# FFN up product as seven block products in a diffusion backbone layer

## Chip, cores and metric

One Trainium2 chip, one core. The time is the device time of one execution in microseconds (us). The kernel before took 1220.67 us, the median of three runs (1220.33 to 1224.66).

## What is computed

One layer on 1024 latent tokens of width 1024, with 256 context tokens. A token mixer comes first: an input projection, then three groups of heads in parallel (a bidirectional state-space scan, a Fourier mix and a pooling mix), and an output projection. A ConvFFN follows. Both are joined to the residual and normalised. The part that the change is about:

```python
def conv_ffn(h, w_up, conv_w, conv_b, w_down, grid):
    a = h @ w_up                                  # 1024 x 1024 @ 1024 x 5632
    a = dwconv2d_grid(a, conv_w, conv_b)          # 3 x 3 per channel on a 16 x 64 grid of tokens
    val, gate = jnp.split(a, 2, axis=-1)          # 2816 channels each
    return (jax.nn.gelu(gate) * val) @ w_down

x = post_norm(x, mix_lat, g1, ln1_g[l], ln1_b[l])
ffn_lat = conv_ffn(modulate(x, sh2, sc2), ...)
x = post_norm(x, ffn_lat, g2, ln2_g[l], ln2_b[l])   # LN(alpha * x + gate * y)
```

In the scan, a chunk of 128 tokens needs, for each of 8 heads and both directions, a 128 x 128 matrix of decays, exp of the difference of two cumulative sums, masked to a triangle and multiplied by C B^T and by dt.

## The kernel before, in words

All products are done in two-part arithmetic: an operand is split into a high part of fewer mantissa bits and a low remainder, and a product is three matmuls, high x high, high x low and low x high. `split` (L214) does it: ScalarE (ACT) writes the high part and GpSimd (POOL), or VectorE (DVE) if named, subtracts to get the low part.

The mixer fills the first 400 us. For every chunk and group of four heads `chunk_pre` (L610) forms C B^T in PSUM, masks it into two triangles (`gt`, L618), multiplies each by dt per head (`U`, L620 and L641), loads the cumulative sums broadcast over partitions (`bc`, L627), subtracts this partition's sum for the two directions and takes the minimum of both (`E`, L629 to L640), takes exp (L642), multiplies (L643) and stores the matrix to DRAM. Output projection, first normalisation (`post1`, L1070) and the transposed, modulated and split input of the FFN (`post2`, L1086) follow. That input lies in SBUF as `h2h` and `h2l`: two halves of 512 tokens, 8 feature tiles of 128.

The FFN goes over 22 channel pairs, each a value tile and a gate tile of 128 channels (L1216). For one tile the weights are loaded and split by `up_weights` (L1119), and 8 features x 3 products x 2 halves = 48 matmuls of 128x512 go into a 128x1024 PSUM tile (L1229). `conv2d` (L1164) takes it from PSUM: one ACT operation for the centre tap and eight DVE operations for the other taps (L1180). After the gate tile come gelu (ACT), the product with the value (POOL) and its split (L1247 to L1249), and the load and split of the pair's rows of the down matrix (L1250 to L1254).

The down product runs between the up products. For every two finished pairs there are 16 units (`down_unit`, L1144), one for each of 8 token tiles and two halves of the output width: 6 matmuls into a 128x512 PSUM tile, whose sum DVE adds to the residual `xa`, which stays in SBUF (L1157, L1159). A unit is put behind every second feature of an up tile (L1231). Nine groups of 16 make 144 units; the last four pairs are a last group, which is multiplied after the last up tile, token tile by token tile (`last_mm`, L1268), and normalised as it is finished (`post_early`, `post_late`).

PSUM has three tiles of 128x1024 (`psa`: the up tiles, later the last group) and two of 128x512 (`psb`: the units). The text gives dependencies and a priority; the order on each engine is fixed ahead of time by a planner that takes what is ready by its own estimates, and at run time each engine keeps that order and waits where an operand isn't there. All DMAs are issued by SyncE (SP), in one queue.

Of the kernel before, what the change touches and what calls it, by code (L numbers as in the profile page):

```python
# [33 lines left out]
def hybrid_layer(  # L34
# [179 lines left out]
    def split(raw, hi, lo, eng=None):  # L214

        S.activation(hi, raw, AF.Identity)  # L216
        (eng or G).tensor_tensor(lo, raw, hi.bitcast(F32), op=ALU.subtract)  # L217
# [262 lines left out]
    dtv, etot, ecs, ncs = (d3(n) for n in ("dtv", "etot", "ecs", "ncs"))  # L480
# [12 lines left out]
    def decay_a(dct):  # L493
# [23 lines left out]
        V.tensor_tensor(dA, dtv, b10(nea[:]), op=ALU.mult)  # L517
        dts.update(dA=dA, cs=cs, tot=tot)

    def decay_b():  # L520
# [12 lines left out]
        V.tensor_scalar(ncs, cs, -1.0, None, op0=ALU.mult)  # L533
# [73 lines left out]
    t12 = mat[:, 1:3, :]  # L607
    ms = nc.dram_tensor("m_scratch", [NT, P, 1024], F32, kind="Internal").ap()

    def chunk_pre(ch, g):  # L610
# [6 lines left out]
        gt = sl.tile([P, 2, P], F32, tag="gt", name=f"gt{ch}{g}")  # L617
        V.tensor_tensor(gt, pg[:, 0:P].unsqueeze(1).broadcast_to([P, 2, P]), t12, op=ALU.mult)  # L618
        f = g * 8
        V.tensor_tensor(U, gt[:, 0, :].unsqueeze(1).broadcast_to([P, 4, P]),  # L620
                        dtv[:, ch, f : f + 4].unsqueeze(2).broadcast_to([P, 4, P]), op=ALU.mult)
        for h in range(4):
            f, b = g * 8 + h, g * 8 + 4 + h
            if h % 2 == 0:
                bc = half("bc", f"bc{ch}{g}{h}", [P, 2, 2, P])
                r = scr[ch * 16 + f : ch * 16 + f + 1, :]
                nc.sync.dma_start(bc, bass.AP(r.tensor, r.offset, [[0, P], [4 * P, 2], [P, 2], [1, P]]))  # L627
                if g == 0:
                    G.tensor_tensor(E[:, h : h + 2, :], bc[:, 0],  # L629
                                    ncs[:, ch, f : f + 2].unsqueeze(2).broadcast_to([P, 2, P]), op=ALU.add)  # L630
                else:
                    for i in range(2):
                        S.activation(E[:, h + i, :], bc[:, 0, i, :], AF.Identity, bias=ncs[:, ch, f + i : f + i + 1])
            if g == 1:
                V.scalar_tensor_tensor(E[:, h, :], bc[:, 1, h % 2, :], ncs[:, ch, b : b + 1], E[:, h, :], op0=ALU.add,  # L635
                                       op1=ALU.min)
            else:
                S.activation(bc[:, 1, h % 2, :], bc[:, 1, h % 2, :], AF.Identity, bias=ncs[:, ch, b : b + 1])
                if h % 2:
                    V.tensor_tensor(E[:, h - 1 : h + 1, :], E[:, h - 1 : h + 1, :], bc[:, 1], op=ALU.min)  # L640
            V.scalar_tensor_tensor(U[:, h, :], gt[:, 1, :], dtv[:, ch, b : b + 1], U[:, h, :], op0=ALU.mult, op1=ALU.add)  # L641
        S.activation(E, E, AF.Exp)  # L642
        G.tensor_tensor(U, U, E, op=ALU.mult)  # L643
# [244 lines left out]
    def chunk_y(ch):  # L888
# [6 lines left out]
                        dcol.unsqueeze(2).broadcast_to([P, 8, 64]), op=ALU.mult)  # L895
# [170 lines left out]
    nc.sync.dma_start(a2r, adar[8:24, :])  # L1066
    xnc = cycle(lambda n: qt("q10", n), lambda n: qt("q11", n), lambda n: post.tile([P, D], F32, tag="p0", name=n))


    def post1(t):  # L1070
# [3 lines left out]
        V.scalar_tensor_tensor(xa[t], xa[t], st[1], lnb, op0=ALU.mult, op1=ALU.add)  # L1074
        st = ln_stats([xa[t]], f"ln2_{t}")
# [51 lines left out]

# [16 lines left out]
    def down_unit(u):  # L1144

        group, t, nb = u
        pt = psb(f"pdn{group[0][0]}_{t}_{nb}")
        n = 3 * len(group)
        i = 0
        s = slice(nb * 512, nb * 512 + 512)  # L1150
        for _, gh, gl, wh, wl in group:
            a, b = gh[:, t * P : (t + 1) * P], gl[:, t * P : (t + 1) * P]
            for u_, v_ in ((a, wh), (a, wl), (b, wh)):
                TE.matmul(pt, u_, v_[:, s], start=i == 0, stop=i == n - 1)  # L1154
                i += 1
        if (t, nb) in seen:
            V.tensor_tensor(xa[t][:, s], xa[t][:, s], pt, op=ALU.add)  # L1157
# [57 lines left out]
    group, queue, acc_v = [], [], None  # L1215
    for n in range(NCT):  # L1216
        ct, i = chan[n], n // 2
        if n > 1 and n + 1 < NCT:
# [192 lines left out]
```

## Time and profile before

| | |
|---|---|
| median of three runs | 1220.67 us |
| the profiled execution | 1225.25 us, span 1223.5 us, mean granted clock 0.983 |
| busy | PE 1158.4, DVE 967.7, POOL 466.3, ACT 383.4 us |
| instructions | PE 5463, DVE 1388, ACT 572, POOL 243 |
| DMA | 122.51 MB |

The profile is one execution. PE is TensorE's matmuls, PEld its weight loads. A row of a timeline gives the start, the time of the merged group, the engine, the line, the operation, the tiles out<-in with their shapes, the count, and in brackets the idle time before it and what ended that. A row of groups gives busy time, mean time of one, and idle time before.

### The profile page before, as it was taken

Reading aid. Unit: us, or ns where it says so; the run is one execution under the profiler, and the core shown is the slowest. Engines: PE = TensorE matmul, PEld = TensorE weight load, DVE = VectorE, ACT = ScalarE, POOL = GpSimd, SP = SyncE. Lnnn points to the kernel's source line nnn. Section 1 sums busy time; section 2 is a strip of 40 time slices with the busy share of each in tenths; the row PEclk is TensorE's granted clock in tenths of the full one; section 3 lists DMA queues with packets and bytes.
Section 4 is the critical chain, followed back from the end, with each engine's and each line's share of the span. In section 5 each row is a group of like instructions: output and inputs, shape, how many; then the busy total and the mean of one; then the engine's idle time right before and its main releaser. Section 6 shows DMA issues by size and latency. Waiting matters only on the chain.

```text
span 1223.5 us, 14330 instructions
## 1 busy us (share of the span) xinstructions
PE 1158.4 (95%) x5463; PEld 941.2 (77%) x5463; DVE 967.7 (79%) x1388; ACT 383.4 (31%) x572; POOL 466.3 (38%) x243
## 2 busy tenths in 40 slices
PE   4999998989978998999999999999999999999996
PEld 2698886767856787788888888888888888888884
DVE  4788799999899889798777777777777777777957
ACT  2263466721443133342221222211222212222144
POOL 0010143353344034674343535343443535353146
PEclk9999998998989999999999999999999999999998
DMA  9848455566526111222021211121121112121013
GB/s 311 293 145 314 156 167 167 162 207 212 198 84 209 43 36 52 69 70 63 24 69 35 69 33 54 35 69 36 35 69 35 52 35 69 35 69 35 18 35 138
DMA packets 104779, 122.51 MB, mean 100 GB/s; under 512 B 7021, under 2 KB 83579, under 8 KB 104711
## 3 DMA queue, kind: packets, MB, share of 16 engines
q1 hardware_dynamic: 104711, 121.60, 31.0%
q8 instruction: 43, 0.70, 0.2%
q14 instruction: 25, 0.20, 0.1%
HBM read 106.82 MB, written 14.76 MB: 99 GB/s over the span
## 4 chain that ended last, share of the span: by engine, by line
PE 75%; DVE 15%; issue 4%; DMA 3%; ACT 1%; POOL 1%; SPq 0%; DVEq 0%; ACTq 0%; POOLq 0%
PE pu L1229 37%; PE pdn L1154 16%; PE pout L1004 4%; PE px L443 4%; PE pz L342 4%; PE pl L1278 3%; PE pu L1190 1%; DVE EU L641 1%; DMA wa<-in_w_ada_dram 1%; DVE EU L635 1%; PE pd L906 1%; DVE st L706 1%; PE pp L443 1%; DVE EU L620 1%; DVE xa L1073 1%
## 5 line engine op out<-in xcount | busy, mean ns | idle before, releaser
L1180 DVE SCALAR_TENSOR_TENSOR cv<-pu,ffc,cv 128x945 f32<-128x945 f32 (+7 forms) x368 | 432.6, 1177 | 20.6 <-ACT cv L1172 10.9
L1229 PE MATMUL pu<-h2l,wuh 128*128 128x512 f32 x656 | 205.6, 394 | 0.0
L1229 PE MATMUL pu<-h2h,wuh 128*128 128x512 f32 x656 | 205.5, 394 | 0.0
L1229 PE MATMUL pu<-h2h,wul 128*128 128x512 f32 x656 | 205.0, 394 | 0.0
L1157 DVE TENSOR_TENSOR xa<-xa,pdn 128x512 f32<-128x512 f32 x128 | 87.4, 683 | 129.0 <-PE pdn L1154 128.7
L217 POOL TENSOR_TENSOR wul<-wur,wuh 128x1024 fp32r<-128x1024 f32 x44 | 106.8, 2427 | 205.1 <-ACT wuh L216 205.1
L1229 PEld LDWEIGHTS pu<-h2h,wul 128*128 128x128 f32 x656 | 123.1, 188 | 29.2
L1229 PEld LDWEIGHTS pu<-h2l,wuh 128*128 128x128 f32 x656 | 123.2, 188 | 29.0
L1229 PEld LDWEIGHTS pu<-h2h,wuh 128*128 128x128 f32 x656 | 123.3, 188 | 28.8
L216 ACT ACTIVATE wuh<-wur 128x1024 fp32r<-128x1024 f32 x44 | 46.3, 1054 | 240.6 <-PE pu L1229 221.8
L1154 PE MATMUL pdn<-wdh,gl 128*128 128x512 f32 x288 | 113.2, 393 | 0.0
L1154 PE MATMUL pdn<-wdl,gh 128*128 128x512 f32 x288 | 113.1, 393 | 0.0
L1154 PE MATMUL pdn<-wdh,gh 128*128 128x512 f32 x288 | 112.8, 392 | 0.0
L1252 POOL TENSOR_TENSOR wdr<-wdr,g2b 128x1024 f32<-128x1024 f32 x22 | 53.0, 2408 | 68.0 <-DMA wdr<-in_ffn_w_down_dram 68.0
L1248 POOL TENSOR_TENSOR cv<-cv,cv 128x1024 f32<-128x1024 f32 (+1 forms) x23 | 53.0, 2306 | 60.4 <-ACT cv L1247 60.3
L217 POOL TENSOR_TENSOR gl<-cv,gh 128x1024 fp32r<-128x1024 f32 (+1 forms) x23 | 53.3, 2317 | 42.4 <-ACT gh L216 42.4
L1154 PEld LDWEIGHTS pdn<-wdl,gh 128*128 128x128 f32 x288 | 54.0, 188 | 12.5
L1154 PEld LDWEIGHTS pdn<-wdh,gh 128*128 128x128 f32 x288 | 54.0, 188 | 12.4
L1154 PEld LDWEIGHTS pdn<-wdh,gl 128*128 128x128 f32 x288 | 54.0, 188 | 12.1
L1172 ACT ACTIVATE cv<-pu,ffc 128x1024 f32<-128x1024 f32 (+3 forms) x46 | 53.1, 1155 | 29.5 <-PE pu L1229 19.3
L1247 ACT ACTIVATE cv<-cv 128x1024 f32<-128x1024 f32 (+1 forms) x23 | 23.5, 1020 | 120.2 <-DVE cv L1180 120.2
L217 POOL TENSOR_TENSOR wdl<-wdr,wdh 128x1024 fp32r<-128x1024 f32 x22 | 52.8, 2415 | 4.7 <-ACT wdh L216 4.7
(351 smaller groups left out, 2124.5 us busy)
## 6 DMA issues: line engine op xcount, KB each, us to landing
wur<-in_ffn_w_up_dram SPq DMA_DIRECT2D x44, 512.0 KB
wad<-in_w_ada_dram SPq DMA_DIRECT2D x32, 512.0 KB
wdr<-in_ffn_w_down_dram SPq DMA_DIRECT2D x22, 512.0 KB
wa<-in_w_ada_dram SPq DMA_DIRECT2D x32, 256.0 KB
bc<-cs_scratch SPq DMA_DIRECT2D x32, 256.0 KB
xr<-in_x_dram SPq DMA_DIRECT2D x8, 512.0 KB
wx_r<-in_w_in_dram SPq DMA_DIRECT2D x8, 512.0 KB
m_scratch<-EU SPq DMA_DIRECT2D x16, 256.0 KB
```

Source lines behind the costliest of these rows:

```text
L216: S.activation(hi, raw, AF.Identity)
L217: (eng or G).tensor_tensor(lo, raw, hi.bitcast(F32), op=ALU.subtract)
L342: TE.matmul(pt[:, j * 512 : j * 512 + ZW], a, b[:, k % 4, :], start=first and i == 0, stop=last and i == 2)
L443: TE.matmul(pt[:, q * 512 : q * 512 + 512], a[:, k, :], b[q][:, k, :], start=k == 0 and i == 0, stop=k == KD - 1 and i == 2)
L1004: TE.matmul(pt[:, nb * 512 : nb * 512 + 512], u, v[:, nb * 512 : nb * 512 + 512], start=first and i == 0, stop=last and i == 2)
L1154: TE.matmul(pt, u_, v_[:, s], start=i == 0, stop=i == n - 1)
L1157: V.tensor_tensor(xa[t][:, s], xa[t][:, s], pt, op=ALU.add)
L1172: S.activation(acc[:, a * 64 : b * 64], pt[:, a * 64 : b * 64], AF.Identity, bias=ffc[:, 396 + ct : 397 + ct], scale=ffc[:, 176 + ct : 177 ...
L1180: last = V.scalar_tensor_tensor(dst, pv[:, r0 + dy : r1 + dy, c0 + dx : c1 + dx], ffc[:, w * 44 + ct : w * 44 + ct + 1], dst, op0=ALU.mult ...
L1229: TE.matmul(pt[:, q * 512 : q * 512 + 512], a[:, k, :], b[q][:, k, :], start=k == 0 and j == 0, stop=k == KD - 1 and j == 2)
L1248: G.tensor_tensor(acc[:, s], acc[:, s], acc_v[:, s], op=ALU.mult)
L1252: G.tensor_tensor(raw, raw, g2b, op=ALU.mult)
```

## The change

From pair 5 on, the up product of a pair is done by Strassen's scheme on six of the eight feature tiles. The 2 x 2 blocks are value and gate channels on one side, features 5 to 7 and 2 to 4 on the other, and the two halves of 512 tokens. Seven block products of 3 features take the place of eight; features 0 and 1 are multiplied as before. The sums of blocks of weights are made by POOL from the raw weights and split (`pair_sums`); those of the input are made once by DVE during pairs 1 to 3 (`combine`) and split, three of them into tiles of their own and the fourth in place of features 5 to 7 of the second half of tokens (`last_t4`). The products are chained in PSUM: ACT copies a partial sum from one bank into another, and later products are added on top of it. Only the seventh product has a PSUM tile of its own, is copied to SBUF and added by DVE.

```diff
+    def first_product(i):
+        pv[i] = psa(f"pu{chan[2 * i]}")
+        X, Z = pv[i][:, 0:512], pv[i][:, 512:1024]
+        mm(X, wk(vw[i], K1), hk(0, K1), True)
+        S.copy(Z, X)
+
+    def pair(i, mid):
+        if i not in pv:
+            first_product(i)
+        X, Z = pv[i][:, 0:512], pv[i][:, 512:1024]
+        mm(X, wk(vw[i], K2), hk(0, K2))
+        slot()
+        mm(Z, sk(i, 2), tk(2))
+        pq[i] = psa(f"pu{chan[2 * i + 1]}")
+        Y, W_ = pq[i][:, 0:512], pq[i][:, 512:1024]
+        S.copy(Y, Z)
+        mm(X, wk(vw[i], 0, KD0), hk(0, 0, KD0))
+        slot()
+        p7 = psb(f"p7_{i}")
+        mm(p7, sk(i, 3), tk(3), True)
+        s7 = post.tile([P, 512], F32, tag="s7", name=f"s7_{i}")
+        S.copy(s7, p7)
+        slot()
+        mm(Z, sk(i, 1), tk(1))
+        seed = S.copy(W_, Z)
...
+        mm(Y, wk(gw[i], K2), hk(1, K1))
+        mm(Z, sk(i, 4), hk(1, K2))
+        if i + 1 < NPAIR:
+            pair_sums(i + 1)
+        mm(Z, wk(vw[i], 0, KD0), hk(1, 0, KD0))
+        slot()
+        acc_v = conv2d(pv[i], chan[2 * i], [(0, 16)])
+        mid()
+        if i + 1 < NPAIR:
+            first_product(i + 1)
+        slot()
+        mm(Y, wk(gw[i], 0, KD0), hk(0, 0, KD0))
+        slot()
+        mm(W_, wk(gw[i], 0, KD0), hk(1, 0, KD0))
...
+        V.tensor_tensor(pqv, pqv, s7.unsqueeze(1).broadcast_to([P, 2, 512]), op=ALU.add)
+        return acc_v
```

`mm` does the three matmuls of each feature into one bank; `slot` puts in one down unit if there is one. Direct pairs keep four slots a tile, a Strassen pair has eight, from pair 3 to the last. The sums of weights and of the input:

```diff
+    def combine(k):
...
+        whole(b11, 0, K1 + k)
+        whole(b12, 1, K1 + k)
+        whole(b22, 1, K2 + k)
+        whole(b21, 0, K2 + k)
+        eng().tensor_tensor(b11, b12, b11, op=ALU.subtract)
+        eng().tensor_tensor(b12, b22, b12, op=ALU.subtract)
+        eng().tensor_tensor(b22, b22, b11, op=ALU.subtract)
+        eng().tensor_tensor(b21, b21, b22, op=ALU.subtract)
+        for j, src in ((0, b11), (1, b22), (2, b12)):
+            split(src, Tt[j][k][:, 0, :], Tt[j][k][:, 1, :], eng())
...
+    def pair_sums(i):
...
+        G.tensor_tensor(a21, a21, a22, op=ALU.add)
+        G.tensor_tensor(a11, a21, a11, op=ALU.subtract)
+        split_s(i, 2, a11)
+        split_s(i, 1, a21)
+        G.tensor_tensor(a12, a12, a11, op=ALU.subtract)
+        split_s(i, 4, a12)
+        G.tensor_tensor(a11, a22, a11, op=ALU.subtract)
+        split_s(i, 3, a11)
```

To make room in SBUF the residual moves to DRAM: `post1` stores it, each unit loads its 128x512 piece into one of three buffers and stores it back, and it is loaded whole for the last group. The down weights are loaded and split in halves of the output width, and the gated product of a pair is formed one pair later (`between`), in two halves.

```diff
     def down_unit(u):
 
         group, t, nb = u
+        xt = post.tile([P, 512], F32, tag="xt", name=f"xt{group[0][0]}_{t}_{nb}", bufs=3)
+        xs = xd[t * P : (t + 1) * P, nb * 512 : nb * 512 + 512]
+        nc.sync.dma_start(xt, xs)
...
         if (t, nb) in seen:
-            V.tensor_tensor(xa[t][:, s], xa[t][:, s], pt, op=ALU.add)
+            V.tensor_tensor(xt, xt, pt, op=ALU.add)
         else:
-            V.scalar_tensor_tensor(xa[t][:, s], xa[t][:, s], ALPHA, pt, op0=ALU.mult, op1=ALU.add)
+            V.scalar_tensor_tensor(xt, xt, ALPHA, pt, op0=ALU.mult, op1=ALU.add)
             seen.add((t, nb))
+        nc.sync.dma_start(xs, xt)
```

In the mixer, the logarithm of dt is put into the exponent, so that `U` needs no products with dt; the lower triangle is chosen by a predicated copy in place of the minimum, and the diagonal is handled with the skip connection. The constant matrices are loaded in two pieces.

```diff
     def chunk_pre(ch, g):
...
+        gt = sl.tile([P, P], F32, tag="gt", name=f"gt{ch}{g}", bufs=2)
+        V.tensor_copy(gt, pg[:, 0:P])
+        gd = sm.tile([P, 1], F32, tag="gd", name=f"gd{ch}{g}")
+        V.scalar_tensor_tensor(junk, pg[:, 0:P], 1.0, ident, op0=ALU.mult, op1=ALU.mult, accum_out=gd)
+        f = g * 8
+        V.scalar_tensor_tensor(skip[:, ch, g * 4 : g * 4 + 4], dtv[:, ch, f + 4 : f + 8], gd, dcol[:, g * 4 : g * 4 + 4],
+                               op0=ALU.mult, op1=ALU.add)
...
+                G.tensor_tensor(bc[:, 1], bc[:, 1], ncs[:, ch, b : b + 2].unsqueeze(2).broadcast_to([P, 2, P]), op=ALU.add)
+            S.activation(E[:, h, :], bc[:, 0, h % 2, :], AF.Identity, bias=ncs[:, ch, f : f + 1])
+            if h % 2:
+                V.copy_predicated(E[:, h - 1 : h + 1, :], below.bitcast(later).unsqueeze(1).broadcast_to([P, 2, P]), bc[:, 1])
         S.activation(E, E, AF.Exp)
-        G.tensor_tensor(U, U, E, op=ALU.mult)
+        V.tensor_tensor(U, E, gt.unsqueeze(1).broadcast_to([P, 4, P]), op=ALU.mult)
         nc.sync.dma_start(ms[ch][:, g * 512 : g * 512 + 512], U.rearrange("p a b -> p (a b)"))
```

More of the change, by code (lines that the diff above doesn't have):

```diff
@@ L478, in b10 @@
         return ap.unsqueeze(1).broadcast_to([P, 10, 16])
-    dtv, etot, ecs, ncs = (d3(n) for n in ("dtv", "etot", "ecs", "ncs"))
+    dtv, etot, ecs, ncs, ldt = (d3(n) for n in ("dtv", "etot", "ecs", "ncs", "ldt"))
     nea = sl.tile([P, 16], F32, name="nea")
@@ L1214, in hybrid_layer @@
     utags = cycle(("wh0", "wl0"), ("wh1", "wl1"))
[L1215 to L1218, printed above, removed]
[L1219 to L1243 removed]
+    TTAG = iter(("q0", "q1", "q8", "q9", "q12", "q14", "q2", "q3", "q4"))
@@ new lines, in pair_gate, with mm @@
+    def pair_gate(i):
+        n = KD - KS
+        wh, wl = qt("X0", f"gwh{i}", [P, n, P], F32R), qt("EM1", f"gwl{i}", [P, n, P], F32R)
+        g = raws.pop(i)[1]
+        split(g[:, 0:n, :], wh[:], wl[:])
+        gw[i] = wh, wl
+    def mm(dst, a, b, start=False):
+        n = len(a)
+        for k in range(n):
+            for j, (u, w) in enumerate(((0, 0), (0, 1), (1, 0))):
+                TE.matmul(dst, a[k][u], b[k][w], start=start and k == 0 and j == 0, stop=k == n - 1 and j == 2,
+                          skip_group_check=True)
@@ L1249, in hybrid_layer @@
             split(acc[:, s], gh[:, s], gl[:, s])
-        raw = ring("ht2", f"wdr{i}")
-        nc.sync.dma_start(raw, w_down[i * P : (i + 1) * P, :])
-        G.tensor_tensor(raw, raw, g2b, op=ALU.mult)
-        wdh, wdl = qt(tg[2], f"wdh{i}", dt=F32R), qt(tg[3], f"wdl{i}", dt=F32R)
-        split(raw[:], wdh[:], wdl[:])
-        group.append((i, gh, gl, wdh, wdl))
-        if len(group) == 2 and i < NPAIR - 3:
-            queue = [(list(group), t, nb) for t in range(NT) for nb in range(2)]
-            group = []
+        gates[i] = gh, gl
@@ new lines, in hybrid_layer, with between @@
+    LASTG = NPAIR - 4
+    accs_ = {}
+    def between(i):
+        j = i - 1
+        if j < 0:
+            return
+        gated(j, *accs_.pop(j))
+        if j < LASTG:
+            if j % 2 == 1:
+                grp = [(m, *gates[m], wds[m]) for m in (j - 1, j)]
+                units.extend((grp, t, nb) for nb in range(2) for t in range(NT))
+                for m in (j - 1, j):
+                    down_raw(m, 1)
+            else:
+                for m in (j, j + 1):
+                    down_raw(m, 0)
+        else:
+            for m in {LASTG: (0,), LASTG + 1: (1,)}.get(j, ()):
+                down_raw(LASTG, m)
+                down_raw(LASTG + 1, m)
@@ L1264, in hybrid_layer @@
         down_unit(u)
+    for t, tag in enumerate(STAG + ("X0", "EM1", "q4", "wh0")):
+        xa[t] = qt(tag, f"xl{t}")
+        nc.sync.dma_start(xa[t], xd[t * P : (t + 1) * P, :])
+    down_split()
+    LT = iter(("q0", "q1", "q8", "q9"))
+    for m in range(LASTG + 2, NPAIR):
+        for nb in range(2):
+            down_weights(m, nb, next(LT))
+    gated(NPAIR - 1, *accs_.pop(NPAIR - 1), tags=("q12", "q14"))
+    group = [(m, *gates[m], wds[m]) for m in range(LASTG, NPAIR)]
     NG = len(group)
```

213 lines of the change are left out of this document (148 added, 65 removed).

## The prediction

> **What bounds the kernel now.** I read the page's chain of waits, then a table of stretches, then the PE and DVE timelines of the FFN, and last the two places where PE is not full.
>
> ```profile
> PE 75%; DVE 15%; issue 4%; DMA 3%; ACT 1%; POOL 1%; SPq 0%; DVEq 0%; ACTq 0%; POOLq 0%
> ```
>
> PE is three quarters of the chain that sets the end. The table of stretches says where (columns: window, length, then PE, PEld, DVE, ACT, POOL busy with instruction counts, granted clock, DMA share, GB/s):
>
> ```profile
> 140.00:205.00 65.00, 60.83 (x311) 51.45 (x310) 59.35 (x95) 39.69 (x66) 21.49 (x21) 0.95 0.62 194
> 205.00:290.00 85.00, 76.01 (x367) 60.86 (x365) 83.59 (x169) 37.17 (x71) 38.86 (x35) 0.98 0.60 194
> 290.00:400.00 110.00, 93.07 (x465) 76.50 (x466) 98.62 (x163) 42.42 (x109) 39.10 (x20) 0.92 0.48 163
> 511.00:1155.00 644.00, 644.00 (x2783) 522.17 (x2782) 487.76 (x470) 150.44 (x143) 287.57 (x120) 1.00 0.17 50
> ```
>
> From 511 to 1155 us, the FFN, PE never idles, at full clock; DVE has 24% to spare and the DMA engines 83%. From 140 to 400 us, the mixer, DVE is the fuller engine (241.6 of 260 us) and PE idles 30 us. So a matmul taken out of the FFN is worth its whole price as long as nothing new makes PE wait, and DVE work taken out of the mixer is worth something, at most PE's idle time.
>
> **The price of a matmul, and the count.** Two timelines of the FFN, PE and DVE:
>
> ```profile
> 801.55 0.63 PE L1229 MATMUL pu<-h2h,wuh 128*128 128x512 f32 x2
> ...
> 804.32 0.40 PE L1154 MATMUL pdn<-wdh,gh 128*128 128x512 f32 x1
> ...
> 805.71 0.63 PE L1229 MATMUL pu<-h2h,wuh 128*128 128x512 f32 x2
> ```
>
> ```profile
> 810.68 3.69 DVE L1180 SCALAR_TENSOR_TENSOR cv<-pu,ffc,cv 128x945 f32<-128x945 f32 x3
> 814.29 0.68 DVE L1157 TENSOR_TENSOR xa<-xa,pdn 128x512 f32<-128x512 f32 x1
> 814.88 3.80 DVE L1180 SCALAR_TENSOR_TENSOR cv<-pu,ffc,cv 128x1008 f32<-128x1008 f32 x3
> 818.60 0.68 DVE L1157 TENSOR_TENSOR xa<-xa,pdn 128x512 f32<-128x512 f32 x1
> 819.20 2.45 DVE L1180 SCALAR_TENSOR_TENSOR cv<-pu,ffc,cv 128x960 f32<-128x960 f32 x2
> ```
>
> From 801.55 to 805.71 PE does 12 up matmuls and the 6 of one down unit: 4.16 / 18 = 0.231 us each. The six of a unit go to one bank one after another (804.32 to 805.71, 1.39 / 6 = 0.232), so the new chains, nine in a row into one bank, should cost no more apiece. A pair now has 2 tiles x 8 features x 3 x 2 halves = 96 up matmuls. A Strassen pair has 7 products x 3 features x 3 = 63, and 4 blocks x 2 remaining features x 3 = 24: 87. Pairs 5 to 21 are Strassen: 17 x 9 = 153 matmuls fewer, 153 x 0.231 = **-35.4 us**. The 144 down units and the last group keep their matmuls. With 8 units (48) a Strassen pair lasts 135 x 0.231 = 31.2 us instead of 33.3.
>
> **Does the rest of a pair fit in 31.2 us?** In the second timeline eight taps last 3.61 + 3.72 + 2.45 = 9.8 us and a unit's sum delays the taps by 0.60; sums are slipped between taps as they become ready, so the order on an engine is by readiness, not by the text. Prices for the rest:
>
> ```profile
> 1174.28 1.29 POOL L217 TENSOR_TENSOR gl<-cv,gh 128x512 fp32r<-128x512 f32 x1 [0.74 <-ACT gh L216]
> ...
> 1179.51 2.41 POOL L217 TENSOR_TENSOR wdl<-wdr,wdh 128x1024 fp32r<-128x1024 f32 x1
> ```
>
> ```profile
> 1185.19 1.22 DVE L1301 TENSOR_TENSOR xa<-xa,pl 128x1024 f32<-128x1024 f32 x1 [12.24 <-PE pl L1278]
> ```
>
> ```profile
> 1194.22 0.57 ACT L1290 COPY pl<-xa 128x512 f32<-128x512 f32 x1
> ```
>
> DVE per pair: 2 x 9.8 + 8 x 0.60 + 1.2 for adding the seventh product = 25.6 us (82%). POOL: eight 128x384 operations (about 1.0 each between the two rows), value low part 2.4, gate low part about 1.6, four halves of down weights and four of the gated product at 1.29: 22.4 us (72%). Neither is the bound. The four PSUM copies on ACT are new waits. Each is bounded below by 0 and above by its copy, 0.57 us and a hand-off, where nothing stands between; but six to thirty matmuls (1.4 to 7 us) stand between each copy and the matmul that needs its bank again. Behind a late copy on ACT wait the other copies and the splits. The tight place is the two-buffer PSUM ring: the third unit of a pair takes the buffer of the second with only the nine matmuls of the seventh product between, 2.1 us, while its sum needs a hand-off of 0.2, the rest of a tap (up to 1.2) and 0.68. That is 0 to 0.6 us a pair; with 0.3, the middle, **+5 us** over 17 pairs (bounds 0 and 10).
>
> **Residual in DRAM.** Each unit gets a 256 KB load and a 256 KB store on SP's queue, 16 more issues a pair. Rows for a 512 KB load (issue, then the operation that waited for it), for a store and for a slow load:
>
> ```profile
> 578.67 0.34 SPq L1251 DMA_DIRECT2D wdr<-in_ffn_w_down_dram  x1
> ```
>
> ```profile
> 582.45 2.40 POOL L1252 TENSOR_TENSOR wdr<-wdr,g2b 128x1024 f32<-128x1024 f32 x1 [3.80 <-DMA wdr<-in_ffn_w_down_dram]
> ```
>
> ```profile
> 189.88 5.17 DMA wf_r<-in_w_in_dram
> ...
> 271.17 2.00 DMA m_scratch<-EU
> ```
>
> Issue to use was 3.8 us, for twice the bytes; a store cost 2.0. A buffer's round is 3.8 + 0.68 + 0.34 + 2.0 = 6.8 us; there are three, and the closest three units of a pair lie 39 matmuls, 9.0 us, apart. So I cost it at nothing: the ring hides it. Traffic: 4 MB a pair is some 130 GB/s on top of 50, where the mixer moved 194 at a 0.62 share. The store of x in the first normalisation adds eight 512 KB issues behind DVE work near 450 us, where DMA is nearly idle: nothing, or 0.34 us each. The split constant and the few small operations on dt (128x160, each under the 0.41 us of L618 below): nothing to 1 us.
>
> **Changeover to Strassen.** The combinations of features are 36 DVE operations on 128x512 (33 in pairs 1 to 3, then 3 that split T4 in place, after the last direct tile). DVE is behind in those pairs already:
>
> ```profile
> 503.16 47.38 DVE L1180 SCALAR_TENSOR_TENSOR cv<-pu,ffc,cv 128x504 f32<-128x504 f32 x41 [4.68 <-ACT cv L1172]
> ```
>
> ```profile
> 609.29 1.19 ACT L1172 ACTIVATE cv<-pu,ffc 128x1024 f32<-128x1024 f32 x1
> ```
>
> It runs taps without a gap from 503. Tile 9, the last direct one, is done at 609.3, with one unit more before it at 610.7. T4 is needed 66 matmuls and one uncovered copy later: 627. DVE until then: 503.2 + 6.0 (rest of tile 0) + 9 x 9.8 + 16 x 0.60 = 607, plus 36 operations. At 0.60 that ends at 628.5; but these read two SBUF operands, and the mixer's groups by line (busy us, mean ns) show what that costs beside POOL:
>
> ```profile
> L641 DVE SCALAR_TENSOR_TENSOR EU<-gt,dtv,EU 128x128 f32<-128x128 f32 x64 | 24.0, 414 | 0.1
> ...
> L620 DVE TENSOR_TENSOR EU<-gt,dtv 128x512 f32<-128x512 f32 x16 | 14.4, 898 | 0.1
> L635 DVE SCALAR_TENSOR_TENSOR EU<-bc,ncs,EU 128x128 f32<-128x128 f32 x32 | 12.1, 414 | 0.0
> L640 DVE TENSOR_TENSOR EU<-EU,bc 128x256 f32<-128x256 f32 x16 | 9.6, 604 | 3.5 <-ACT cvc L558 1.7 <-POOL EU L629 1.0 <-ACT bc L638 0.9
> L618 DVE TENSOR_TENSOR gt<-pg,mat 128x256 f32<-128x256 f32 x16 | 6.6, 414 | 0.1
> L706 DVE TENSOR_TENSOR st<-st,etot 128x512 f32<-128x512 f32 x7 | 5.9, 843 | 0.4 <-DMA m_scratch<-EU 0.4
> ...
> L709 DVE TENSOR_TENSOR st<-st,pst 128x512 f32<-128x512 f32 x7 | 4.6, 677 | 0.0
> ```
>
> The same 128x512 size takes 843 ns with two SBUF operands (L706) and 677 with one in PSUM (L709): 0.17 more, so 0.77 each, ending at 634.5. PE waits **+7 us**; bounds 1 (no contention) and 21 (first rival). The Trainium skill, "SBUF — State Buffer", section "SBUF: two separate sides", says that such a DVE operation and a GpSimd one exclude each other for the whole instruction. This rule speaks against the change: by it the time is the first rival's.
>
> **Mixer.** Lines 641, 620, 635, 640 and 618 above are what a chunk's preparation costs DVE, and they all go: 24.0 + 12.1 + 9.6 + 6.6 + 14.4 = 66.7 us. In their place, sixteen times: a 128x128 copy (under L618's 0.41), a 128x128 product with a sum (0.41), a tiny one (under 0.2), two predicated copies of 128x256 and one 128x512 product (0.90 as L620). No row shows a predicated copy: 0.42 if like L618, 0.60 if like L640, both of its size; I take 0.5, the middle. About 2.8 in all, 16 x 2.8 = 45 us: DVE is relieved of 22, and a predicated copy would have to take 1.2 us before it gained work. POOL loses the 128x512 product and keeps the additions; ACT keeps its count. PE idles 13 us from 140 to 290 and 17 from 290 to 400, so the worth lies between 0 and 22 us; half, **-11 us**, since the chunk chain also waits for loads and for PE.
>
> **Tail.** Now PE has nine left-over units and the last group as cover after the last up matmul:
>
> ```profile
> 1154.57 12.44 PE pdn L1154 x54
> 1167.01 38.99 PE pl L1278 x168
> ```
>
> ```profile
> 1154.67 0.78 ACT L1172 ACTIVATE cv<-pu,ffc 128x512 f32<-128x512 f32 x1 [9.04 <-PE pu L1229]
> ```
>
> ```profile
> 1167.73 5.22 DVE L1180 SCALAR_TENSOR_TENSOR cv<-pu,ffc,cv 128x512 f32<-128x512 f32 x7
> ```
>
> After the change pairs 3 to 20 use all 18 x 8 = 144 slots: those 12.4 us of cover are gone (the work is only earlier). Pair 21's value taps start 12 matmuls before PE's end and finish 8.2 us after it; then the sum 1.2, ACT 0.8, eight half-tile taps 8 x 5.22 / 7 = 5.9, gelu 0.6 (as the copy above), POOL 1.3, ACT 0.6, POOL 1.3: the first gated half is there at 20 us. PE has till then 72 matmuls, of which 18 need the buffer that the gate taps hold: 12.5 us. It waits **+8 us** (0 if the order is kinder; 13 in the order of the text).
>
> **Sum.** -35.4 + 5 + 7 - 11 + 8 = -26.4 us. The profiled execution took 1225.25 us (span 1223.5 and 1.75 around it), 4.6 above the median of 1220.67; it becomes 1198.9, the median 1194.
>
> **Rivals.** *The lock at the changeover.* POOL is 45% busy with 2.4 us instructions in the FFN; a DVE operation that waits for half of one costs 0.45 x 1.2 = 0.54 more, 1.14: T4 is ready at 648, 21 us late instead of 7: 1208. For it: 843 against 677. Against: in the mixer only 0.17 was lost.
> *More than that.* All 22 us of the mixer count and the tail loses 2: 1177. For: DVE leads there for 260 us. Against: PE's own 230 us.
> *The saving is eaten.* The mixer gives nothing, the tail costs 13, POOL (72%, in bursts of sums, gated product and splits) brings a pair's low parts 0.8 us late: -35.4 + 7 + 13 + 14 = -1: 1219, no change. For: eight more POOL operations a pair stand ahead of products. It is also the case in which the change doesn't do what it says.
> *The ring of residual buffers runs dry: slower.* If loads and stores land in the 5.2 us of the slow row, a round is 5.2 + 0.68 + 0.34 + 5.2 = 11.4 against 9.0: 2.4 us for each of 18 pairs, 43 in place of the 5: 1232. DVE stands at the sum, its taps queue behind it and PE waits for PSUM. It turns the sign once a landing passes 4.9 us (31 us lost). For: SP issues in order, and a load that waits for a buffer holds the stores behind it. Against: the store's 2.0 us. The Trainium skill, "DMA: Bandwidth & Descriptors", section "Anatomy of one DMA — SWDGE (gpsimd) path", fits 2.0 us plus bytes / 436e3, for another issuing path; by it, as an estimate, 256 KB land in 2.6 us and the ring hides them.
>
> **Chances and range.** Forecast (1184 to 1204) 0.53, lock 0.13, more 0.14, eaten 0.10, ring 0.10. Less than 0.5% (6 us) can't be told from no change, so faster 0.80, same 0.10, slower 0.10. The range 1174 to 1218 leaves out the ring, the far end of "more" and part of "eaten".
>
> **What would show it.** Right: 5310 PE instructions; a steady Strassen pair of 31 to 32 us; DVE near 82% there; PE idle of 5 to 10 us near 630 and after the last up product; the stretch to 290 us shorter by about 10. Wrong: DVE waiting for the residual load (ring), combinations above 1 us each (lock), PE waiting for POOL's low parts (eaten), or a pair of 34 us or more.

## The result and the profile after

The changed kernel takes 1260.44 us (median of 4 runs, 1253.3 to 1263.81) where the kernel before takes 1220.73 beside it: a ratio of 1.0294, 95% interval 1.0262 to 1.0327. It is slower by 2.9%, and the forecast of 1194 was wrong in sign. The profiled execution took 1259.02 us (span 1257.2).

Two lines of the page of the changed kernel, busy times and the chain of waits:

```profile
PE 1143.0 (91%) x5310; PEld 915.6 (73%) x5310; DVE 991.8 (79%) x1413; ACT 463.7 (37%) x787; POOL 595.1 (47%) x465
...
PE 43%; DVE 19%; DMA 16%; POOL 11%; issue 5%; ACT 5%; SPq 1%; POOLq 0%; DVEq 0%; ACTq 0%
```

The 153 matmuls are gone (5310 in place of 5463), yet PE's share of the chain fell from 75% to 43%: DMA (3 to 16%), POOL (1 to 11%), ACT (1 to 5%) and DVE now stand between matmuls that used to follow each other. The table of stretches (columns as in the prediction) shows where PE idles:

```profile
610.00:640.00 30.00, 26.05 (x104) 20.19 (x103) 28.50 (x33) 9.56 (x17) 11.62 (x10) 0.94 0.33 106
640.00:648.00 8.00, 3.26 (x14) 2.05 (x12) 6.98 (x7) 2.28 (x4) 6.34 (x5) 1.00 0.39 128
...
700.00:800.00 100.00, 94.94 (x404) 74.79 (x403) 71.45 (x73) 35.64 (x56) 68.72 (x56) 1.00 0.52 169
```

PE was full from 511 to 1155 us before; now it lacks 5 of 100 us in the steady pairs and more at the changeover. How long a pair lasts is read from the convolutions' starts on ACT, one for each finished tile. Four of them in the changed kernel's ACT timeline: the first tile, the last direct tile, the first value tile by Strassen (pair 5) and that of pair 20:

```profile
498.19 0.81 ACT L1195 ACTIVATE cv<-pu,ffc 128x576 f32<-128x576 f32 x1
...
620.42 1.19 ACT L1195 ACTIVATE cv<-pu,ffc 128x1024 f32<-128x1024 f32 x1
...
656.18 1.19 ACT L1195 ACTIVATE cv<-pu,ffc 128x1024 f32<-128x1024 f32 x1
...
1164.43 1.21 ACT L1195 ACTIVATE cv<-pu,ffc 128x1024 f32<-128x1024 f32 x1 [0.86 <-PE pu L1315]
```

This gives three lengths, used for every run below: *direct*, first to last direct tile, 620.42 - 498.19 = 122.2 us (before: 107.0 from 502.31 to 609.29); *changeover*, 656.18 - 620.42 = 35.8; *pair*, (1164.43 - 656.18) / 15 = 33.88, longer than the 33.3 of a plain pair, where 135 matmuls of 0.231 make 31.2.

### The profile page after: what moved, and what is told of

The parts are those of the page before. It is cut to its first block, busy times and chain, and to the rows that moved or that the text cites. A ratio compares the mean times of both kernels' runs of the same rounds, so it can differ in the third digit from the quotient of the medians.

```text
span 1257.2 us, 15177 instructions
## 1 busy us (share of the span) xinstructions
PE 1143.0 (91%) x5310; PEld 915.6 (73%) x5310; DVE 991.8 (79%) x1413; ACT 463.7 (37%) x787; POOL 595.1 (47%) x465
## 4 chain that ended last, share of the span: by engine, by line
PE 43%; DVE 19%; DMA 16%; POOL 11%; issue 5%; ACT 5%; SPq 1%; POOLq 0%; DVEq 0%; ACTq 0%
PE pu L1315 13%; PE pdn L1176 7%; DMA x_scratch<-xt 4%; PE pout L1010 4%; DVE cv L1203 4%; PE px L445 4%; PE pz L344 4%; PE p L1315 2%; DMA wdr<-in_ffn_w_down_dram 2%; POOL wdr L1395 2%; DMA wur<-in_ffn_w_up_dram 2%; PE pl L1517 2%; POOL cv L1421 2%; POOL gl L219 2%; DMA xt<-x_scratch 1%
## 5 line engine op out<-in xcount | busy, mean ns | idle before, releaser
L1176 PE MATMUL pdn<-wd,gh 128*128 128x512 f32 x576 | 185.5, 399 | 9.7 <-DVE xt L1181 8.9
L1176 PEld LDWEIGHTS pdn<-wd,gh 128*128 128x128 f32 x576 | 107.9, 189 | 38.5 <-DVE xt L1181 10.2
L1179 DVE TENSOR_TENSOR xt<-xt,pdn 128x512 f32<-128x512 f32 x128 | 87.3, 682 | 50.2 <-DMA xt<-x_scratch 26.8
L1176 PE MATMUL pdn<-wd,gl 128*128 128x512 f32 x288 | 115.0, 399 | 8.7 <-POOL gl L219 8.7
L1315 PE MATMUL pu<-h2h,wuh 128*128 128x512 f32 x170 | 71.0, 418 | 19.7 <-ACT pu L1347 11.4
L1315 PE MATMUL pu<-T,S 128*128 128x512 f32 x306 | 76.0, 392 | 0.0
L219 POOL TENSOR_TENSOR S<-wur,S 128x384 fp32r<-128x384 f32 x68 | 69.3, 1021 | 13.9 <-ACT S L218 13.9
L218 ACT ACTIVATE S<-wur 128x384 fp32r<-128x384 f32 x68 | 35.3, 520 | 101.6 <-POOL wur L1293 56.5
L1315 PE MATMUL pu<-h2l,wuh 128*128 128x512 f32 x170 | 67.7, 398 | 0.0
L1315 PE MATMUL pu<-h2h,wul 128*128 128x512 f32 x170 | 67.7, 398 | 0.0
L1315 PEld LDWEIGHTS pu<-T,S 128*128 128x128 f32 x306 | 57.4, 188 | 12.9
L1315 PEld LDWEIGHTS pu<-h2h,wuh 128*128 128x128 f32 x170 | 32.5, 191 | 37.1 <-ACT pu L1347 16.9
```

Source lines behind the costliest of these rows:

```text
L219: return (eng or G).tensor_tensor(lo, raw, hi.bitcast(F32), op=ALU.subtract)
L1176: TE.matmul(pt, u_, wd[nb][:, v_, :], start=i == 0, stop=i == n - 1)
L1179: V.tensor_tensor(xt, xt, pt, op=ALU.add)
L1315: TE.matmul(dst, a[k][u], b[k][w], start=start and k == 0 and j == 0, stop=k == n - 1 and j == 2, skip_group_check=True)
```

## The experiments

Theories, in the order in which they came up. First: two raw weight buffers let the next value weights land late, and their splits at the heads of ACT's and POOL's queues hold the PSUM copies. Rival: the residual's trip through DRAM (its load and store in every unit) holds DVE and PE. Third: the combinations of features on DVE exclude POOL and come too late. A fourth ("new") on SP's order came out of the first runs. Each ratio is against the kernel before, run beside it, with its 95% interval; the changed kernel's 1.0294 is the mark, and 0.01 is 12.2 us.

**Order of the value split.** The next pair's value split behind the pair's third copy:

```diff
-            pair_value(i + 1)
+            with tc.issue_after(seed.ins):
+                pair_value(i + 1)
```

> One thing moved: the split of the next pair's value weights stands behind the pair's third PSUM copy on ACT's queue (and its low part correspondingly on POOL's), where it stood ahead of the first one. First theory (two raw weight buffers: the value weights land late, and their split holds ACT's and POOL's queues): the copies, conv starts and gated products no longer stand behind a split that waits for its load, the steady pair falls from 33.9 to about 32 us, 16 x 1.9 = 30 us less: 1230 (1222 to 1240). Rival (residual round trip through DRAM holds DVE): the pair stays at 33.5 to 34.3, the time at 1252 to 1266. If the cycle load, split, sums, next load is itself what lasts a pair, the later split makes it longer: above 1266.

Measured: 1340.19 us, 1.0939 (1.0917 to 1.0961), pair 39.3. The first theory's cure made it much worse, as the last sentence of the expectation allowed. I read it so: the split is wanted early, since the sums and the next load hang on it. In this kernel SP waits 134.3 us for POOL's sums before weight loads (640 to 1240 us), where the changed kernel waits 56.7.

**A third raw buffer.** Fourth weight sum into the spare third of the gate weights' tiles, the freed tile as a third buffer:

```diff
+                rings["ht2"] = ("wr0", "wr1", "EM0")
```

> A third buffer for the raw up weights from pair 6 on (S4 is put into unused parts of the gate weights' tiles, which frees one tile); nothing is left out. First theory: the raw loads no longer wait for POOL's last sum of the pair before, so the value weights are there when their split comes up on ACT; the waits of ACT (101.5 us in all) and POOL (72.3) for the raw load go, the pair falls to 31.3 to 32.5 us: 1220 to 1240. Rival (residual trip): weights are there earlier but DVE still waits for the residual: pair 33.3 to 34, 1248 to 1262.

Measured: 1258.95, 1.0264 (1.0244 to 1.0285), pair 33.76. ACT's 101.5 us of waiting for the raw load are gone but for 4.1; ACT's waits in this kernel (engine, line, releaser: us in total, times, longest) show what came in their place:

```profile
ACT S L218 <- PE pu L1322: 55.4, 14, 5.8
...
ACT sideX L218 <- PE pu L1322: 48.6, 19, 4.8
```

Its splits now wait for PE to release the tiles of sums, and the kernel is hardly faster. The first theory falls: a big wait on an engine off the path was not a loss.

**No trip.** The residual's load and store left out of a unit:

```diff
-        nc.sync.dma_start(xt, xs)
-            V.tensor_tensor(xt, xt, pt, op=ALU.add)
+            V.tensor_tensor(xt, g2b[:, s], pt, op=ALU.add)
-        nc.sync.dma_start(xs, xt)
```

> Left out: the load and the store of the residual in every unit; DVE adds the product to a vector that lies in SBUF all along, so the sums over the groups are left out too, with the same instructions on PE and DVE. Rival (residual trip): DVE's 26.5 us of waits for the residual loads go, and SP has nothing behind which a weight load waits: the pair falls to 31.3 to 32 us, 1205 to 1225 in all. First theory (raw weight buffers): the weight load still waits for POOL's last sum and lands 4.4 us later, the splits still stand at the heads of their queues; only SP's order is relieved: 1240 to 1258, a pair of 33 us or more.

Measured: 1240.89, 1.0127 (1.0109 to 1.0145), pair 32.68: 0.0167, 20 us, and 1.2 us a pair. The time is at the foot of the second expectation, the pair between the two; the trip, which I had costed at nothing, costs. Where it reaches PE is seen in PE's waits of the changed kernel in the steady pairs (640 to 1160 us):

```profile
PE pu L1315 <- ACT pu L1347: 11.4, 8, 3.0
PE pdn L1176 <- POOL gl L219: 8.7, 7, 1.3
PE pu L1315 <- ACT pu L1336: 8.4, 9, 1.2
```

Without the trip the three are 3.7, 6.9 and 3.8 us. So most of what PE waits less came through ACT's copies. The copy at L1347 writes a PSUM tile that DVE's taps still read: it waits 57.4 us for them, 23.8 without the trip. With a third raw buffer as well, made in the place of residual buffers:

> Left out: the residual's loads and stores, and with them the sums over the groups; besides, the raw up weights have three buffers from pair 6 on. Without the trip alone a pair lasts 32.7 us, with the third raw buffer alone 33.8. If the two wait beside each other (each hides the other's removal), both together give a pair of 31.4 to 32.2 and 1218 to 1232. If the raw buffer costs nothing at all: 32.5 to 32.9 and 1236 to 1245. What stays then is on ACT's and POOL's queues.

Measured: 1251.24, 1.0226 (1.0205 to 1.0246), pair 33.21: worse than without the buffer. Neither expectation held.

**The trip alone**, in the kernel before:

```diff
+        xt = post.tile([P, 512], F32, tag="xt", name=f"xt{group[0][0]}_{t}_{nb}", bufs=3)
+        nc.sync.dma_start(xt, xs)
-            V.tensor_tensor(xa[t][:, s], xa[t][:, s], pt, op=ALU.add)
+            V.tensor_tensor(xt, xt, pt, op=ALU.add)
+        nc.sync.dma_start(xs, xt)
```

> The kernel before, with nothing changed but the residual in DRAM: the same ring of three, loads and stores in all down units and one load of all of it for the last group. If the trip holds DVE and PE by itself (250.9 us of SP waiting for a store to land before the next load): 10 to 25 us more than before, 1230 to 1246, as the removal in the changed kernel gave 20 back. If it costs only together with Strassen's shorter and uneven spacing of units (here they stand every 12 matmuls, 4.2 us apart): within 5 us of before.

Measured: 1264.18, 1.0343 (1.0316 to 1.0371): 42 us by the trip alone, more than expected, though its units stand 18 matmuls apart. SP's timeline in this kernel shows how:

```profile
800.14 0.32 SPq L1151 DMA_DIRECT2D xt<-x_scratch  x1
800.55 0.38 SPq L1166 DMA_DIRECT2D x_scratch<-xt  x1
803.86 0.32 SPq L1151 DMA_DIRECT2D xt<-x_scratch  x1
804.27 0.38 SPq L1166 DMA_DIRECT2D x_scratch<-xt  x1
807.38 0.32 SPq L1151 DMA_DIRECT2D xt<-x_scratch  x1
```

Load and store come in twos, 3.5 to 3.7 us apart: a load (L1151) is issued only when the store before it, 3.1 to 3.3 us earlier, has landed, because it takes that store's buffer, and the next store stands behind it in SP's order. So SP can't do a unit in less than a landing and two issues, 3.5 to 3.7 us of the 4.16 in which PE does one, and the weight loads stand in the same queue. SP's and DVE's waits, first in this kernel, and PE's from 511 to 1155 us:

```profile
SPq L1151 <- DMA x_scratch<-xt: 365.2, 111, 5.1
...
DVE xt L1162 <- DMA xt<-x_scratch: 162.1, 61, 8.7
...
PE pdn L1159 <- DVE xt L1162: 20.6, 10, 4.9
```

and SP's in the changed kernel:

```profile
SPq L1169 <- DMA x_scratch<-xt: 250.9, 95, 5.5
SPq L1136 <- POOL S L219: 56.7, 16, 5.5
```

SP stands in 365.2 and 250.9 us for landings; DVE's sums wait for loads 162.1 us in the first, up to 8.7 at a time, and PE waits for these sums. Some 31 of the 42 us are lost before the last up product, the rest after it. The new theory: it is the place of the load on SP's queue, not the length of the ring.

**Longer ring, then later loads.** Five buffers (the freed tile holds two), the loads left where they were:

```diff
+        j = xturn[0] % 5
+        if more and j > 2:
+            return more[0][:, j - 3, :]
```

> Five residual buffers instead of three from pair 5 on (in the tile that S4 leaves free). If the trip costs because a load waits until the store three units before has landed (250.9 us of SP's waits): the pair falls from 33.9 to 32.7 to 33.1, as without the trip, 1240 to 1247. If it costs through SP's order (a weight load that waits for POOL stands ahead of residual loads and stores), or through the traffic: 33.6 to 33.9, 1254 to 1260.

Measured: 1254.74, 1.0259 (1.0238 to 1.028), pair 33.65: almost nothing, and SP waits as before, in this kernel's row:

```profile
SPq L1179 <- DMA x_scratch<-xt: 260.9, 94, 5.6
```

As I read it, the scheduler hoists each load as far as the ring permits, that is right behind the store that frees its buffer, however long the ring is. So, with five buffers, each load behind the store of three units before:

```diff
+        with tc.issue_after(stores[-3].ins) if len(stores) >= 3 else ExitStack():
+            nc.sync.dma_start(xt, xs)
```

> The kernel before with only the residual in DRAM, as in the run of the trip alone (1264, 42 us over before), but with five buffers and each load behind the store of three units before. New theory (SP held by a load that waits for the store just ahead of it): at most a quarter of the 42 us stays, 1222 to 1234. If the traffic or the round trip itself costs: 1250 or more.

Measured, in the kernel before: 1225.11, 1.0006 (0.9987 to 1.0025). The 42 us are gone with the same traffic (169 to 179 GB/s in the table of stretches). SP's waits there:

```profile
SPq L1169 <- DVE xt L1165: 189.3, 79, 3.4
...
SPq L1154 <- DMA x_scratch<-xt: 5.7, 7, 1.5
```

Landings hold the units' loads for 5.7 us; SP now waits for DVE's sums, as it should. Order and ring length were changed together here; the ring alone was tried only in the changed kernel. There the same pair of edits:

> Five residual buffers as before, and each residual load placed on SP's queue behind the store of three units before, where it stood directly behind the store that frees its buffer. New theory: a load that directly follows the store whose buffer it takes holds SP until that store has landed (2.6 us each, at any ring length), and later stores and the weight loads queue behind it; now the store it needs lies two units back: SP's 260.9 us of such waits fall under 60, the pair from 33.6 to 32.4 to 32.9, 1232 to 1245. If the time goes to the traffic itself: no change, 1250 to 1258.

Measured: 1248.24, 1.0208 (1.0177 to 1.0238), pair 33.17: 10 us, half of what leaving out the trip gives; SP's waits for stores fell to 8.3, but its largest is now a weight load that waits for POOL:

```profile
SPq L1136 <- POOL sideEM L219: 155.7, 30, 7.5
...
SPq L1182 <- DMA x_scratch<-xt: 8.3, 7, 1.5
```

> The changed kernel with its three buffers; only each load is placed behind the store of two units before, so that one store lies between it and the store that it needs. New theory: part of the gain of five buffers, as the needed store has one unit's time (3.9 us) to land: SP's waits for stores about 100 us instead of 250.9, 1242 to 1252. If the order on SP doesn't matter: 1254 to 1260; if a later load only makes the sums wait: above 1260.

Measured, with `stores[-2]` and three buffers: 1258.53, 1.0293 (1.0258 to 1.0327), pair 33.64. SP's waits for stores fell to 63.4 and nothing was gained: a miss. In the changed kernel SP's waits are not all of it.

**No combinations.** The 36 operations left out, the products take the features as they are:

```diff
-                    combine(i - 1)
-                last_t4()
-        return [(t[:, 0, :], t[:, 1, :]) for t in Tt[j - 1]]
+        return hk(j % 2, (K1, K2, K1)[j - 1])
```

> Left out: all 36 combinations of the features on DVE (the products take the features as they are instead; same matmuls). Third theory (they share SBUF with POOL): t9 falls back from 620.4 by 12 to 14 us, the first two Strassen values lose another 5 to 14 us of waiting; the steady pairs stay at 33.9: 1232 to 1242. If they were covered by PE after all: t9 at 615 or later and the total above 1250.

Measured: 1233.76, 1.0067 (1.0043 to 1.0091): 28 us; direct 108.1, changeover 26.2, pair 33.43. The largest single loss, and it lies where expected. Its ten runs spread from 1225.43 to 1238.43, and the profiled one is the fastest: the 28 us go by the medians and are good to some 5 us either way. PE's two waits on the direct tiles of the changed kernel, which are gone in this one:

```profile
559.98 1.19 PE L1466 MATMUL pu<-h2h,wuh 128*128 128x512 f32 x2 [2.65 <-DVE cv L1203]
...
590.18 1.22 PE L1176 MATMUL pdn<-wd,gh 128*128 128x512 f32 x2 [5.82 <-DVE xt L1181]
```

Taps and units' sums are late on DVE. After each wait PE is slow for some microseconds more (last section). DVE's and POOL's timelines of the changed kernel over one set of combinations:

```profile
536.39 1.28 DVE L1254 TENSOR_TENSOR ta<-h2h,h2l 128x512 f32<-128x512 f32 x2
537.59 1.79 DVE L1254 TENSOR_TENSOR tb<-h2h,h2l 128x512 f32<-128x512 f32 x1
539.30 1.77 DVE L1254 TENSOR_TENSOR t4r<-h2h,h2l 128x512 f32<-128x512 f32 x1
541.00 1.79 DVE L1261 TENSOR_TENSOR ta<-ta 128x512 f32<-128x512 f32 x1
542.71 1.19 DVE L1203 SCALAR_TENSOR_TENSOR cv<-pu,ffc,cv 128x945 f32<-128x945 f32 x1
543.82 0.68 DVE L1262 TENSOR_TENSOR ta<-tb,ta 128x512 f32<-128x512 f32 x1
544.42 2.89 DVE L219 TENSOR_TENSOR T<-ta,T 128x512 fp32r<-128x512 f32 x1
547.24 0.68 DVE L1263 TENSOR_TENSOR tb<-tb,ta 128x512 f32<-128x512 f32 x1
```

```profile
537.21 3.31 POOL L1421 TENSOR_TENSOR cv<-cv,cv 128x512 f32<-128x512 f32 x2 [4.77 <-ACT cv L1420]
540.49 3.46 POOL L219 TENSOR_TENSOR gl<-cv,gh 128x512 fp32r<-128x512 f32 x2
543.90 2.87 POOL L219 TENSOR_TENSOR wul<-wur,wuh 128x1024 fp32r<-128x1024 f32 x1
```

The same operation takes 0.68 us while POOL idles and 1.77 to 2.89 beside it, and the two engines take turns (POOL's 128x512 operation, 1.29 in the prediction's row, is 1.65 here). The tap at 542.71, with one operand in PSUM, keeps its 1.19. Of the 36 operations 13 are lengthened, by 16.0 us in all: 36 x 0.60 + 16.0 = 37.6, 1.05 each. Now POOL's work on the direct pairs left out (low parts of weights and gates, gated product):

```diff
+        if 0 < direct[0] and ct not in (chan[2 * PS], chan[2 * PS + 1]):
+            anchor[0] = S.copy(wh[:], raw[:])
+            return wh, wh
```

> The changed kernel; in the direct pairs 1 to 4 POOL's low parts of the up weights and of the gates and its gated product are left out (the high parts stand in for them, with the same matmuls). If POOL's operations exclude DVE's with two operands in SBUF: of the 13 combinations that took 1.3 to 2.9 us at most 4 stay long, DVE gets 10 to 14 us back, 1242 to 1250 in all. If the 36 operations cost by their count: they stay as they are, 1253 to 1260.

Measured: 1239.57, 1.0131 (1.0114 to 1.0148): 20 us; direct 107.4, changeover 35.6. DVE's timeline over the same operations:

```profile
535.78 0.68 DVE L1258 TENSOR_TENSOR tb<-h2h,h2l 128x512 f32<-128x512 f32 x1
536.39 0.68 DVE L1258 TENSOR_TENSOR t4r<-h2h,h2l 128x512 f32<-128x512 f32 x1
536.99 0.68 DVE L1265 TENSOR_TENSOR ta<-ta 128x512 f32<-128x512 f32 x1
```

All are at 0.68, and the direct tiles keep their pace with the 36 operations in place. Exclusion, not count, cost the direct pairs their 14 us (the run takes POOL's own work away too, but PE waited nowhere for POOL there in the changed kernel). Spreading them, from pair 7 on:

```diff
-    KS, PS = 3, 5
+    KS, PS = 3, 7
-            if 0 < i <= KS:
+            if i in (1, 3, 5):
```

> Strassen from pair 7 instead of 5, and the three combinations of features after pairs 1, 3 and 5 instead of 1, 2 and 3; 18 matmuls more. Third theory (36 operations of about 1.0 us on top of 73 us of DVE work do not fit into three pairs of 33.3 us): DVE has 5 x 33.3 = 166 us for 122 + 38, direct tiles come at their pace, the 28 us that leaving out the combinations gave come back but for 3 to 8: 1234 to 1242, as the two pairs cost 33.3 instead of 33.9. If it is the changeover itself (weights, T4) that costs: 1250 or more.

Measured: 1250.86, 1.0229 (1.0208 to 1.0251): 8 us, a third of what was expected; the 14 direct tiles still lose time and the changeover is 37.7. With the five buffers and late loads:

> Five buffers and late loads, and besides Strassen from pair 7 with the combinations after pairs 1, 3 and 5 (18 matmuls more). The spread alone gave 8 us; with SP free the weights of the changeover come in time too (there PE waited 9.5 us for copies behind a split that waited for its load): 10 to 18 us less than the run with five buffers and late loads, 1218 to 1232. If the changeover's loss isn't SP's: 5 to 9 less.

Measured: 1239.37, 1.0137 (1.0107 to 1.0167), pair 32.99: 9 us less than without the spread, the second expectation (changeover 33.6 after 37.7 with the spread alone, so SP has a small part in it at most); the best version that keeps the whole computation and Strassen, still slower than before. With three operations behind each tile instead of eleven in a run, in the version with the spread, the five buffers and the late loads:

> The run with five buffers, late loads and Strassen from pair 7, in which the combinations' 33 operations stand three at a time behind each direct tile instead of eleven in a run. If the block is what costs (units' sums queue behind it and PE waits for PSUM): 5 to 10 us less than that run, 1226 to 1234 against a before of 1222 to 1225. If exclusion beside POOL alone is what costs: within 3 us of it, 1236 to 1242.

Measured: 1243.97, 1.0167 (1.0152 to 1.0183). Not better: the direct tiles came 3.8 us sooner, but the last combinations were then done only at the changeover, which grew to 44.8.

**What stays of the changeover.** ACT's timeline of the changed kernel there, and the matmul after the wait:

```profile
640.03 1.06 ACT L218 ACTIVATE wuh<-wur 128x1024 fp32r<-128x1024 f32 x1 [4.32 <-DMA wur<-in_ffn_w_up_dram]
641.00 0.57 ACT L1353 COPY s<-p 128x512 f32<-128x512 f32 x1
644.67 0.52 ACT L218 ACTIVATE S<-wur 128x384 fp32r<-128x384 f32 x1 [3.11 <-POOL wur L1293]
647.78 0.52 ACT L218 ACTIVATE S<-wur 128x384 fp32r<-128x384 f32 x1 [2.58 <-POOL wur L1298]
648.21 0.58 ACT L1356 COPY pu<-pu 128x512 f32<-128x512 f32 x1
```

```profile
648.84 0.79 PE L1315 MATMUL pu<-h2h,gwh 128*128 128x512 f32 x1 [5.58 <-ACT pu L1356]
```

The next pair's splits stand ahead of this pair's last copy and wait for a load and for POOL; PE waits 5.58 us for the copy. In the kernel without combinations the copy stands first, and PE's longest wait there is 2.0. With POOL idle on the direct pairs the same copy still holds PE for 5.56 us, so exclusion isn't what makes the changeover long. That it is this order and nothing else wasn't tried by itself.

**Both out, and the sums too.**

> Left out: the combinations and the residual's loads and stores. If the two losses lie in different places (direct pairs and changeover; steady pairs): 28 + 20 us less than the changed kernel, 1203 to 1213, that is 10 to 18 under before. If they hide each other: 1215 to 1228. What is then missing of the forecast 26 us is the pair's other waits, the tail and the mixer.

Measured, without combinations and trip: 1217.24, 0.9944 (0.9927 to 0.9961). 43 us of the expected 48: the two losses nearly add. Changeover 26.0, pair 32.44. Then the weight sums left out as well, alone and beside the two:

```diff
-        G.tensor_tensor(a21, a21, a22, op=ALU.add)
...
-        return [(sw[i][j][:, 0, k, :], sw[i][j][:, 1, k, :]) for k in range(KS)]
+        return wk(gw[i], K2) if j == 3 else wk(vw[i], K2 if j == 1 else K1)
```

> Combinations, residual trip and sums of weights all left out; what stays is the order of the products, the four PSUM copies, the units and the tail. If the three account for the loss: a pair of 31.3 to 31.8, 1190 to 1202. If the products' order and the copies cost by themselves: 32 or more a pair, 1206 to 1217.

Measured: 1217.19, 0.9944 (0.9924 to 0.9965), pair 32.70: the sums cost nothing once the others are gone. It is the second expectation: with all three out, most of the forecast saving is still missing. PE's row for 700 to 1100 us:

```profile
700.00:1100.00 400.00, 383.04 (x1639) 306.10 (x1638) 304.13 (x306) 117.19 (x169) 171.02 (x122) 1.00 0.16 50
```

PE still idles 17 of 400 us, by its waits for unit sums (10.2) and one of the copies (6.8).

> The changed kernel without the sums of weights: eight operations of POOL and four splits of ACT a pair are left out, and the products take the weights' splits as they are; same matmuls, combinations and residual kept. If the weights' chain load, split, sums, next load holds a pair: 33.9 falls to 32.5 to 33.2, and 5 to 10 us of the changeover come back: 1228 to 1246. If SP held by the residual's loads sets the pair: 33.4 or more, 1247 to 1258.

Measured: 1309.59, 1.0698 (1.0656 to 1.0741), pair 37.2: 50 us slower than the changed kernel with less work, against both expectations. In its PE waits one copy stands out:

```profile
PE pu L1305 <- ACT pu L1337: 33.3, 11, 3.8
...
ACT pu L1337 <- DVE cv L1203: 70.8, 11, 7.1
```

It is the copy at L1347 of the changed kernel, and it waits for DVE's taps, which still read the PSUM tile that it writes. Why the taps became so late wasn't settled; the queues' order is another one when the sums are missing.

**The mixer alone**, in the kernel before (the diff's part in `chunk_pre`):

> The kernel before with only the mixer's new preparation of a chunk. Forecast: 11 us less (0 to 22), 1204 to 1216 against a before of 1220 to 1225. By the first direct tile of the changed kernel, which came 4.1 us earlier: 3 to 6 less. DVE's relief of 22 us is seen in the stretch 140 to 290 in either case.

Measured: 1218.57, 0.9957 (0.994 to 0.9974): 5 us less. DVE's busy time from 140 to 290 us is the third number pair of each row, first before, then with the new mixer:

```profile
140.00:290.00 150.00, 136.83 (x676) 112.31 (x674) 142.95 (x263) 76.86 (x136) 60.35 (x55) 0.97 0.61 194
```

```profile
140.00:290.00 150.00, 138.85 (x718) 116.15 (x717) 123.29 (x240) 76.29 (x136) 50.47 (x55) 0.99 0.66 206
```

DVE is relieved of 19.7 us, near the 22 forecast, and PE gains 2.0 busy us in the stretch. This is the only whole version here that beats both kernels.

## Why the prediction was wrong

- **Matmuls, -35.4: right** in count and price (5310; 0.23 us each at full clock).
- **Residual in DRAM, 0: wrong**, the first failed step. "The ring hides it" compared a round of 6.8 us with 9.0 between units and left out that a load holds SP until the store ahead of it has landed. Leaving the trip out gives 20 us here; alone it costs 42. The rival of the dry ring had the place and even the sentence ("SP issues in order"), but put the price on a landing above 4.9 us and gave it one chance in ten; landings of 3.3 us were enough, and a ring of five didn't help. With the order on SP mended, half of the 20 us stayed in the changed kernel; where that half goes is open. The Trainium skill, "DMA: Bandwidth & Descriptors", section "Anatomy of one DMA — SWDGE (gpsimd) path", says that a semaphore wait happens on the issuing sequencer before dispatch; SP's 250.9 us of waits agree.
- **Changeover, +7: wrong**, the second. The price of an operation was 1.05 us, not 0.77, nearly the 1.14 of the lock rival. The trace before had the price: I read the row of L706 up to 275 us, where 7 of its 14 operations lie. From 205 to 290 us it is

```profile
L706 DVE TENSOR_TENSOR st<-st,etot 128x512 f32<-128x512 f32 x14 | 15.4, 1108 | 0.4 <-DMA m_scratch<-EU 0.4
```

That is 0.43 us more than the 676 ns with an operand in PSUM (L709, the same stretch), so 1.03 each. The place was wrong as well: I let the combinations delay only T4. T4 was done at 632.2, before the forecast 634.5, and no wait of PE names it; but taps and units' sums queue behind the combinations on DVE, and the direct tiles slow down by 14 us. Without them the kernel is 28 us faster. The Trainium skill's page "SBUF — State Buffer", section "SBUF: two separate sides", has the rule; the rows at 537 to 547 us agree with it.
- **Steady pair, +5: too small.** Without combinations and trip a pair is 32.44, 1.2 above 31.2: 17 x 1.2 = 20. I costed only the PSUM ring of the units, and in the changed kernel PE waited 0.8 us in all for their sums from 640 to 1160 us. The copies, which I let six to thirty matmuls cover, and the low parts of the gated product, the sign of the "eaten" rival, hold PE instead (the rows under *No trip*).
- **Mixer, -11: half.** 5 us alone; DVE's relief came nearly as forecast, but most of it was covered.
- **Tail, +8: right.** From the last up product to the end 63.4 us, against 56.5 before without the left-over units: 7.
- **The sum** in its own terms: -35.4 + 20 + 20 + 28 - 5 + 7 = +35 us; measured 0.0294 x 1220.7 = 36. That it fits so well is partly luck: without combinations and trip the same terms give -13, and that run measured -7; the two together gave 43, not 48. These gaps cancel.

## What to carry to other kernels

A transfer that waits for its buffer holds everything behind it on its queue: place a reload behind stores that are long landed, with buffers enough for that, and look at the issuing queue's own waits before calling a round trip hidden. Cost an operation with two SBUF operands by what POOL does beside it in that very stretch, and count whom it delays in its queue, not only who needs its result. A stage where PE never idled has no slack to pay for new hand-offs: of the 2.1 us that a pair's nine matmuls saved, waits took 1.2 even without combinations and trip.

## What the runs showed that I had not expected

After a wait PE is slow for a while. Waits of 1.3 us in the steady pairs leave the granted clock at 1.00; after the 5.58 us above, matmuls start every 0.43 us instead of 0.23, and the clock of the next stretch in the changed kernel is

```profile
648.00:652.00 4.00, 3.16 (x8) 2.54 (x9) 0.00 (x0) 2.27 (x5) 3.58 (x4) 0.57 0.09 16
```

Waits of 2.65 and 3.00 us in this kernel had the same effect: 0.84 in the 10 us from 560, 0.60 in the 4 us from 676. In the run without the sums alone a wait of 2.47 us was enough:

```profile
862.00:868.00 6.00, 5.88 (x19) 4.73 (x20) 5.18 (x6) 0.30 (x2) 0.00 (x0) 0.73 0.60 215
```

Six matmuls at 0.43 us there add half of the wait again. The Trainium skill, "TensorE: Matmul & The Clock Gate", section "Part 1: The HAM clock gate", puts the fall of the clock behind an idle window of about 3.4 us; here the shorter wait did it too.
